# Down projection cut into steps between the next pair's gate_up chunks, in a mixture-of-experts loop on one core

## The chip, the core and the metric

One Trainium2 chip, one of its cores. A core has TensorE (PE: matmuls, and PEld: its weight loads), VectorE (DVE), ScalarE (ACT), GpSimd (POOL) and SyncE (SP), which here only issues transfers. The metric is the device time of one execution in microseconds, as the median of several runs; a profiled execution gives the trace, whose span is a little shorter than the execution's time.

## The reference

A decoder layer on 272 tokens (256 and 16 meta tokens) of width 2048: a mixer (mLSTM and sparse attention), then a hierarchical mixture of experts. Only the second half is touched by the change:

```python
h = layer_norm(ALPHA * h + mix, ln1_g, ln1_b)
# router: a group of 4, then the top 2 of its 8 experts: 32 experts, 2 per token
def run_block(args):
    toks, ws, e = args
    xb = x2[toks]
    gu = xb @ w_gate_up[e]                         # 2048 -> 1024
    hb = silu(gu[:, :D_FF]) * gu[:, D_FF:]         # 512
    return (hb @ w_down[e]) * ws[:, None]          # 512 -> 2048
...
h = layer_norm(ALPHA * h + ffn, ln2_g, ln2_b)
return h[:, N_META:]
```

All weights are float32: 8 MB of gate_up and 4 MB of down per expert, 403 MB for 32 experts, each used once.

## The kernel before

Only the 256 tokens that reach the output go through the experts. Each expert takes up to 64 rows (a loop behind the main one serves an expert with more, and runs only if there is one).

**Loads.** `specs` lists 386 loads in the order of use: for each pair of experts 16 gate_up chunks (256 rows of the weight, 1 MB each, `g`), then 8 down chunks (a quarter of an expert, 1 MB each). SP issues them (line 808) in a ring of 14 slots named by the tags of tiles that are dead by then (x0 to x3, y0 to y3, m0 to m3, u0, u1); two early chunks go into the accumulator's room instead. `issue()` issues the next load as soon as the slot that it takes has been used; `next_w()` hands out the next chunk.

**One pair of experts.** `expert_up` runs twice: 8 chunks, in each 2 values of k, and for each k two matmuls of 64 columns by 512, one into each half of the array's columns (lines 1078 and 1080). A float32 matmul is two instructions in the trace ("passes"). Behind the eighth chunk ScalarE applies silu (L1084), VectorE multiplies (L1085, `hb`), four transposes of 64 rows bring hb's columns to partitions (L1088, `ph`), and ScalarE copies them (L1091, `hT`). Then down runs for both experts, one into each half of the columns (L1242, `py`, four PSUM banks, 4 x 4 x 2 matmuls). The four results wait in `pend`; `flush(1)` behind each of the next chunks takes one: scaled by the gate into a high and a low part (L1231 `yh`, L1232 `yl`), scattered to tokens by a one-hot matmul (L1186, `pc`) and added to `acc` by VectorE (L1192): the combine.

**Around it.** `dispatch(q)` gathers the rows of four experts by one-hot matmuls into `xe` (L1002, evacuated by L1006 and L1009), ahead of every second pair; `slots_of` makes the one-hot of the way back. `add_residual(n)` adds a quarter of the residual in each of pairs 1 to 4, `final_scale` makes the last norm's scale during the last expert; both broadcast a row of 512 with `bcast_cols`: four diagonal matrices on VectorE and four matmuls with ones (L1104). `final_rows_load`, `final_masks` and `final_rows` prepare constants of the last norm. The last pair's down goes by columns (LASTP, L1254), each part combined at once, then the norm and eight output transfers.

**Order.** A list scheduler of the framework puts the instructions of each engine in order before the run: it takes the ready instruction that is first in the program, by its own estimate of times. An engine's queue is then run strictly in that order, so a matmul that isn't ready holds up those behind it.

## Time and profile before

| | us |
|---|---|
| runs | 1804.3, 1806.74, 1811.79; median 1806.74 |
| the profiled execution | 1807.82 |
| its span in the trace | 1806.1 |
| PE busy | 1718.2 (95%) |
| VectorE, ScalarE, GpSimd busy | 711.8, 455.6, 111.0 |
| loads of gate_up, 1 MB each: issue to landing, median | 15.0 |

The span is what the trace covers; 1.7 us of the execution lie outside of it. The busy time of PE counts overlapped passes once. The expert loop begins at about 816 us.

### The profile page before, as it was taken

To read this page: it belongs to the slowest core of one execution; us is meant where nothing else is said; L and a number is where in the kernel's file an instruction comes from. 1 tells how busy PE (TensorE), PEld (TensorE's weight loads), DVE (VectorE), ACT (ScalarE), POOL (GpSimd) and SP (SyncE) were. 2 spreads that over 40 slices of the span, in tenths; PEclk is the share of its full clock that TensorE was granted. 3 is DMA by queue.
4 is the path that set the end of the run, shared out by engine and by line. 5 is a ranking of instruction groups with operands and counts; after the bars stand their busy time and mean duration, and the time that the engine had idled before them with its cause. 6 is when DMAs were issued, how large, how long until landed. Compare 5 with 4: busy or idle time off the path is not lost. (4 is left out here: it accounts for less than half of the span.)

```text
span 1806.1 us, 21173 instructions
## 1 busy us (share of the span) xinstructions
PE 1718.2 (95%) x8626; PEld 1043.8 (58%) x8626; DVE 711.8 (39%) x1204; ACT 455.6 (25%) x703; POOL 111.0 (6%) x131
## 2 busy tenths in 40 slices
PE   8599999999999999999999999999999999999996
PEld 7598899988787877874343343333433434334332
DVE  7356774454556456552232242122112221222024
ACT  5243444444343444342010110110101101101010
POOL 3000210001122022000000000000000000000002
PEclk8799999999999999999999999999999999999998
DMA  7634454447565568458999999999999999999992
GB/s 219 129 117 142 141 164 140 148 156 247 173 213 173 198 217 295 171 212 343 419 403 408 413 356 421 421 391 421 421 420 420 422 420 421 420 422 420 421 402 71
DMA packets 155925, 538.67 MB, mean 298 GB/s; under 512 B 15772, under 2 KB 64116, under 8 KB 107680
## 3 DMA queue, kind: packets, MB, share of 16 engines
q1 hardware_dynamic: 153120, 530.54, 76.4%
q0 software_dynamic: 2640, 6.72, 1.9%
q8 instruction: 69, 1.13, 0.3%
q14 instruction: 32, 0.26, 0.0%
q10 hardware_dynamic: 64, 0.02, 0.0%
HBM read 533.50 MB, written 3.74 MB: 297 GB/s over the span
## 5 line engine op out<-in xcount | busy, mean ns | idle before, releaser
L1078 PE MATMUL gu<-we,xe 128*64 128x512 f32 x1016 | 455.9, 597 | 0.0
L1080 PE MATMUL gu<-we,xe 128*64 128x512 f32 x1016 | 454.5, 597 | 0.0
L1242 PE MATMUL py<-we,hT 128*64 128x512 f32 x960 | 276.8, 611 | 0.0
L1078 PEld LDWEIGHTS gu<-we,xe 128*64 128x64 f32 x1016 | 131.7, 137 | 244.2 <-issue 230.1
L1085 DVE TENSOR_TENSOR hb<-gu,hb 64x512 f32<-64x512 f32 x32 | 22.0, 689 | 349.1 <-ACT hb L1084 349.1
L1242 PEld LDWEIGHTS py<-we,hT 128*64 128x64 f32 x960 | 82.1, 137 | 123.8 <-issue 113.5
L1080 PEld LDWEIGHTS gu<-we,xe 128*64 128x64 f32 x1016 | 131.5, 137 | 17.2 <-issue 16.1
L1084 ACT ACTIVATE hb<-gu 64x512 f32<-64x512 f32 x32 | 18.9, 591 | 422.5 <-PE gu L1080 422.5
L1192 DVE TENSOR_TENSOR acc<-pc,acc 128x512 f32<-128x512 f32 (+1 forms) x122 | 77.5, 677 | 76.3 <-PE pc L1186 76.3
L1231 ACT ACTIVATE yh<-py,gsl 128x512 fp32r<-128x512 f32 (+1 forms) x65 | 42.7, 679 | 255.4 <-PE py L1242 178.7
L1232 DVE SCALAR_TENSOR_TENSOR yl<-py,gsl,yh 128x512 fp32r<-128x512 f32 (+1 forms) x65 | 46.7, 736 | 139.1 <-ACT yh L1231 138.7
L1009 DVE TENSOR_SCALAR xe<-pxe,gbp 128x256 f32<-128x256 f32 x64 | 34.8, 544 | 111.3 <-PE pxe L1002 111.3
L1002 PEld LDWEIGHTS pxe<-oh,uh 128*128 128x128 f32 x256 | 40.6, 197 | 48.3 <-DVE xe L1009 27.9
L1186 PE MATMUL pc<-yh,ohT 128*128 128x512 f32 (+1 forms) x130 | 53.9, 438 | 14.5 <-DVE acc L1192 11.6
L1006 ACT ACTIVATE xe<-pxe,gbp 128x256 f32<-128x256 f32 x64 | 36.0, 563 | 106.9 <-PE pxe L1002 106.9
L1002 PE MATMUL pxe<-oh,uh 128*128 128x256 f32 x256 | 59.6, 315 | 2.0 <-DMA acc<-in_w_gate_up_dram 2.0
L1178 POOL TENSOR_TENSOR fin<-acc,fin 128x512 f32<-128x512 f32 (+1 forms) x10 | 10.3, 1052 | 785.7 <-DVE acc L1192 785.7
L1186 PEld LDWEIGHTS pc<-yh,ohT 128*128 128x128 f32 x130 | 23.0, 188 | 55.6 <-issue 37.5
L1002 PE MATMUL pxe<-oh,ul 128*128 128x256 f32 x256 | 52.1, 285 | 0.0
L1186 PE MATMUL pc<-yl,ohT 128*128 128x512 f32 (+1 forms) x130 | 51.3, 418 | 0.8 <-DVE yl L1232 0.7
L1088 PEld LDWEIGHTS ph<-ident,hb 64*128 64x128 f32 x128 | 17.8, 210 | 44.3 <-DVE hb L1085 43.5
L1002 PEld LDWEIGHTS pxe<-oh,ul 128*128 128x128 f32 x256 | 41.1, 199 | 0.0
(920 smaller groups left out, 3109.7 us busy)
## 6 DMA issues: line engine op xcount, KB each, us to landing
we<-in_w_gate_up_dram SPq DMA_DIRECT2D x254, 1024.0 KB, 15.0
we<-in_w_down_dram SPq DMA_DIRECT2D x126, 1024.0 KB, 13.2
gm_r<-in_w_in_dram SPq DMA_DIRECT2D x16, 1024.0 KB, 5.0
ga_r<-in_w_in_dram SPq DMA_DIRECT2D x16, 1024.0 KB, 5.1
wo_r<-in_w_out_dram SPq DMA_DIRECT2D x16, 1024.0 KB, 5.1
qk_r<-in_w_in_dram SPq DMA_DIRECT2D x8, 1024.0 KB, 6.4
mv_r<-in_w_in_dram SPq DMA_DIRECT2D x8, 1024.0 KB, 5.3
aq_r<-in_w_in_dram SPq DMA_DIRECT2D x8, 1024.0 KB, 5.2
```

The lines of the kernel that those rows point to most:

```text
L1002: nc.tensor.matmul(pt[:, :4 * C], lhsT=part[:, b, rows_of(k)], rhs=ohf[:, b], start=i == 0 and b == 0, stop=i == 1 and b == 1)
L1006: nc.scalar.activation(xe[:, k], pt[:, :4 * C], AF.Identity, bias=gbp[:, 1, k:k + 1], scale=gbp[:, 0, k:k + 1])
L1009: nc.vector.tensor_scalar(xe[:, k], pt[:, :4 * C], gbp[:, 0, k:k + 1], gbp[:, 1, k:k + 1], op0=ALU.mult, op1=ALU.add)
L1078: nc.tensor.matmul(pg_[other], lhsT=lt, rhs=w[:, kk, 0:512], start=k == 0, stop=k == KD - 1)
L1080: nc.tensor.matmul(pg_[mine], lhsT=lt, rhs=w[:, kk, 512:1024], start=k == 0, stop=k == KD - 1)
L1084: nc.scalar.activation(hb[mine], pg_[other], AF.Silu)
L1085: nc.vector.tensor_tensor(hb[mine], pg_[mine], hb[mine], op=ALU.mult)
L1186: nc.tensor.matmul(pc[:, :n], lhsT=ohT[:, b * P:b * P + P], rhs=y[:, :n], start=i == 0, stop=i == 1)
L1192: nc.vector.tensor_tensor(av, pc[:, :n], av, op=ALU.add)
L1231: nc.scalar.activation(yh[:, :n], py[:, :n], AF.Copy, scale=gate)
L1232: nc.vector.scalar_tensor_tensor(yl[:, :n], py[:, :n], gate, yh[:, :n].bitcast(F32), op0=ALU.mult, op1=ALU.subtract)
L1242: nc.tensor.matmul(pys[c][i * 64:i * 64 + 64], lhsT=hTs[i][:, kk], rhs=ws[i][:, 0, c * 512:c * 512 + 512], start=kk == 0, stop=kk == 3)
```

## The change

- `specs` becomes a dictionary. From the second pair on, two down chunks of the pair before stand ahead of every fourth gate_up chunk.
- The ring becomes a free list: a chunk's slot is returned by `used()` when its last matmul is written, and the next load takes the oldest free slot. There are still 14 slots; the final scale and the constants no longer take slots of the ring, except one.
- `expert_up` is split. In the loop over 16 chunks of a pair: a chunk (`up_chunk`), then one sixteenth of the down of the pair before (`down_step`, two matmuls; none behind the first chunk, two behind the last), then a combine if two results wait (or in the first two chunks).
- The transposes are done once per pair for both experts (`up_turn`, 128 rows), behind the first chunk of the next pair.
- `dispatch` stands behind all of a pair's chunks, `slots_of` behind the eleventh chunk of every second pair.
- Rows of ln1 and ln2 are loaded after the first pair, split in two parts after the second, and broadcast with one matmul each (`bcast_rows`, 9 rows, float32r) instead of four diagonals and four matmuls. `add_residual` moves one pair later; `final_scale` moves behind the last chunk.

```diff
-    specs = []
-    for e0 in range(0, NE, 2):
-        for e in (e0, e0 + 1):
-            specs += [(w_gu[e, kc * 256:kc * 256 + 256].rearrange("(p k) c -> p k c", k=2), 2, 1024)
-                      for kc in range(8)]
-        if e0 + 2 < NE:
-            specs += [(w_dn[e].rearrange("(p k) c -> p k c", k=4)[:, kk:kk + 1], 1, D)
-                      for kk in range(4) for e in (e0, e0 + 1)]
-        else:
-            specs += [(w_dn[e, :, c0:c0 + n].rearrange("(p k) c -> p k c", k=4), 4, n)
-                      for c0, n in LASTP for e in (e0, e0 + 1)]
-    slots = [(big, t) for t in XT]
+    specs = {}
+    for p in range(NE // 2):
+        for n in range(16):
+            if p and n % 4 == 0:
+                kk = n // 4
+                for e in (2 * p - 2, 2 * p - 1):
+                    specs["d", e, kk] = (w_dn[e].rearrange("(p k) c -> p k c", k=4)[:, kk:kk + 1],
+                                         1, D)
+            e, kc = 2 * p + n // 8, n % 8
+            specs["g", e, kc] = (w_gu[e, kc * 256:kc * 256 + 256]
+                                 .rearrange("(p k) c -> p k c", k=2), 2, 1024)
+    for c0, n in LASTP:
+        for e in (NE - 2, NE - 1):
+            specs["l", e, c0] = (w_dn[e, :, c0:c0 + n].rearrange("(p k) c -> p k c", k=4), 4, n)
+    todo = deque(specs)
+    ndone = len(todo)
+    free = deque((big, t) for t in XT)
     live = {}
+    home = {}
     extra = {}
-    order = []
-    state = {"issued": 0, "used": 0}
-
-    def slot_tile(shape, name, r, dt=F32):
-        pool, tag = slots[r % NSLOT]
-        return pool.tile(shape, dt, name=name, tag=tag, bufs=1)
 
     def issue(n=None):
 
-        while state["issued"] < (len(specs) if n is None else n):
-            i = state["issued"]
-            r = len(order)
-            if i not in extra and r >= NSLOT and order[r - NSLOT] >= state["used"]:
+        while todo and (n is None or ndone - len(todo) < n):
+            key = todo[0]
+            if key not in extra and not free:
                 break
-            src, a, b = specs[i]
-            if i in extra:
-                w = extra[i]().rearrange("p (a b) -> p a b", a=a)
+            todo.popleft()
+            src, a, b = specs[key]
+            if key in extra:
+                w = extra[key]().rearrange("p (a b) -> p a b", a=a)
             else:
-                order.append(i)
-                w = slot_tile([P, a, b], f"we{i}", r)
+                home[key] = pool, tag = free.popleft()
+                w = pool.tile([P, a, b], F32, name="we" + "_".join(map(str, key)), tag=tag, bufs=1)
             nc.sync.dma_start(out=w, in_=src)
-            live[i] = w
-            state["issued"] = i + 1
-
-    def next_w():
-        i = state["used"]
-        state["used"] = i + 1
-        return live.pop(i)
-
-    NSLOT = 4 + 4 + 4 + 2
+            live[key] = w
+
+    def used(*key):
+
+        live.pop(key)
+        if key in home:
+            free.append(home.pop(key))
+
     ta_ctx.close()
-    slots += [(big, t) for t in YT] + [(mx, t) for t in MT] + [(up, t) for t in UT]
+    free += [(big, t) for t in YT] + [(mx, t) for t in MT]
+    NSLOT = len(free)
...
+    extra.update({("g", 1, NSLOT - 8 + i): lambda i=i: in_acc(i) for i in range(2)})
+    issue(NSLOT + 2)
+    free += [(up, t) for t in UT]
...
-    def expert_up(e, xe, hb):
+    hTs = {}
+
+    def up_chunk(e, kc, xe, pg_):
...
+        used("g", e, kc)
...
-        pt = pdt(f"ph{e}")
+
+    def up_turn(p, hb):
+
+        pt = pdt(f"ph{p}")
         for kk in range(4):
-            nc.tensor.transpose(pt[:, kk * C:kk * C + C], hb[mine, kk::4],
-                                ident[mine, mine])
-        hT = me.tile([P, 4, C], F32, name=f"hT{e}", tag="hT", bufs=2)
-        nc.scalar.copy(hT, pt[:, :256].rearrange("p (a b) -> p a b", a=4))
-        return hT
+            nc.tensor.transpose(pt[:, kk * P:kk * P + P], hb[:, kk::4], ident)
+        hT = me.tile([P, 4, P], F32, name=f"hT{p}", tag="hT", bufs=1)
+        nc.scalar.copy(hT, pt.rearrange("p (a b) -> p a b", a=4))
+        hTs[p] = hT
+
+    def down_step(p, kk, c, py):
+
+        for i in range(2):
+            nc.tensor.matmul(py[i * 64:i * 64 + 64], lhsT=hTs[p][:, kk, 64 - i * 64:128 - i * 64],
+                             rhs=live["d", 2 * p + i, kk][:, 0, c * 512:c * 512 + 512],
+                             start=kk == 0, stop=kk == 3)
+        if c == 3:
+            for i in range(2):
+                used("d", 2 * p + i, kk)
...
-    def bcast_cols(c0, name):
-
+    def bcast_rows(m, n, name):
+
+        dg = me.tile([P, P], F32R, name=f"{name}d", tag="dg", bufs=2)
+        nc.vector.tensor_copy(dg, mk[:, m:m + 1].to_broadcast([P, P]))
         pt = pdt(name)
-        for c in range(4):
-            dg = me.tile([P, P], F32, name=f"{name}d{c}", tag="dg", bufs=2)
-            nc.vector.tensor_scalar(dg, ident, col[:, c0 + c:c0 + c + 1], None, op0=ALU.mult)
-            nc.tensor.matmul(pt[:, c * P:c * P + P], lhsT=ones, rhs=dg, start=True, stop=True)
+        r = slice(32 * n, 32 * n + 9)
+        nc.tensor.matmul(pt, lhsT=dg[r], rhs=gr[r], start=True, stop=True)
...
-            nc.scalar.copy(fin[0][:, n * 512:n * 512 + 512], bcast_cols(104 + 4 * n, f"pg2{n}"))
+            nc.scalar.copy(fin[0][:, n * 512:n * 512 + 512], bcast_rows(2, n, f"pg2{n}"))
...
-    def final_rows_load():
+    mk = cst([P, 5], "mk")
...
-            for r, m, a in ((0, 3, ln2_g), (3, 2, ln2_b)):
+            for r, m, a in ((0, 3, ln2_g), (3, 2, ln2_b), (5, 2, ln1_g), (7, 2, ln1_b)):
...
+        mr = cst([P, 9], "mr")
+        for r in range(9):
+            late(nc.vector.tensor_reduce(mr[:, r:r + 1], idr[:, r], axis=AX.X, op=ALU.add))
+        late(nc.vector.tensor_tensor(mk[:, 0:1], mr[:, 1:2], mr[:, 4:5], op=ALU.add))
+        for r in (6, 8):
+            late(nc.vector.tensor_tensor(mk[:, 0:1], mk[:, 0:1], mr[:, r:r + 1], op=ALU.add))
+        for i, r in ((2, 0), (3, 5), (4, 7)):
+            late(nc.vector.tensor_tensor(mk[:, i:i + 1], mr[:, r:r + 1], mr[:, r + 1:r + 2],
+                                         op=ALU.add))
...
-    def final_rows():
+    def rows_split():
+        nonlocal gr
         h = me.tile([P, 512], F32R, name="grh", tag="yh")
-        gr = slot_tile([P, 512], "gr", NORD + 3, F32R)
+        gr = me.tile([P, 512], F32R, name="gr", bufs=1)
...
-    for pr_ in range(NE // 2):
-        e0 = 2 * pr_
-        q = pr_ // 2
...
+    turn = []
+    for p in range(NE // 2):
+        e0 = 2 * p
+        if p:
+            pys = [pyp.tile([P, 512], F32, name=f"py{p - 1}_{c}", tag="py") for c in range(4)]
+        steps = deque((kk, c) for kk in range(4) for c in range(4) if p)
+        for n in range(16):
+            e, kc = e0 + n // 8, n % 8
+            if kc == 0:
+                pg_ = pgu.tile([P, 512], F32, name=f"gu{e}", tag="gu")
+            up_chunk(e, kc, xe, pg_)
+            while turn:
+                turn.pop()()
+            for _ in range(0 if n == 0 else 1 if n < 15 else 2):
+                if steps:
+                    kk, c = steps.popleft()
+                    down_step(p - 1, kk, c, pys[c])
+                    if kk == 3:
+                        pend.append(lambda c=c, py=pys[c], f=gated_of(p - 1, cur):
+                                    f(c * 512, 512, py))
+            issue()
+            if n == 10 and p % 2:
+                cur = slots_of(p // 2, ohf)
+            if len(pend) > 1 or n < 2:
+                flush(1)
+            if n == 7:
+                hb = me.tile([P, 512], F32, name=f"hb{p}", tag="hb", bufs=1)
+            if kc == 7:
+                up_end(e, pg_, hb)
+            if n == 15:
+                turn.append(lambda p=p, hb=hb: up_turn(p, hb))
+        if p == 0:
+            prepare()
+            rows_load()
+            row_masks()
+        if p % 2:
+            q = p // 2
+            if p == LAST:
+                while turn:
+                    turn.pop()()
+                flush()
+            if q + 1 < NE // 4:
+                xe, ohf = dispatch(q + 1)
+        if p == 1:
+            rows_split()
+        if 2 <= p < 6:
+            add_residual(p - 2)
+
+    pool, tag = next(f for f in free if f[1] not in XT)
+    fin.append(pool.tile([P, D], F32, name="fin0", tag=tag, bufs=1))
+    f12 = me.tile([P, 2, D], F32, name="fin12", tag="xe", bufs=1)
+    fin += [f12[:, 0], f12[:, 1]]
+    final_scale()
...
```

## Rows read from the trace of the kernel before

**Rows 1.** The page: busy time of each engine, its share of the span and its instructions.

```profile
PE 1718.2 (95%) x8626; PEld 1043.8 (58%) x8626; DVE 711.8 (39%) x1204; ACT 455.6 (25%) x703; POOL 111.0 (6%) x131
```

**Rows 2.** Busy time by stage of the expert loop: start and end in us, length, busy us of PE, of PE's weight loads, VectorE, ScalarE and GpSimd, granted clock, DMA share, GB/s.

```profile
842.00:930.00 88.00, 87.45 (x397) 35.92 (x395) 19.08 (x37) 10.52 (x19) 0.00 (x0) 1.00 1.01 420
930.00:1000.00 70.00, 68.05 (x278) 25.51 (x276) 25.01 (x51) 6.51 (x11) 4.18 (x8) 0.98 1.00 397
1000.00:1070.00 70.00, 67.64 (x309) 28.35 (x305) 22.79 (x43) 9.75 (x17) 0.00 (x0) 1.00 0.97 389
1070.00:1140.00 70.00, 67.65 (x282) 25.07 (x284) 21.67 (x42) 4.57 (x8) 0.00 (x0) 1.00 1.01 411
1140.00:1210.00 70.00, 67.89 (x306) 27.49 (x302) 13.98 (x23) 9.66 (x17) 0.00 (x0) 1.00 0.99 401
1210.00:1700.00 490.00, 473.59 (x2082) 185.96 (x2082) 101.57 (x175) 55.86 (x99) 0.00 (x0) 1.00 1.01 421
```

**Rows 3.** Waits from 800 us to the end: engine, what and line, what it waited for, then us in total, times, longest us.

```profile
PEld gu L1078 <- DMA we<-in_w_gate_up_dram: 7.1, 24, 0.4
PE ph L1088 <- DVE hb L1085: 16.3, 29, 0.7
```

**Rows 4.** The load queue (SP, line 808) from 1700 to 1726 us: the issues with first and last start, and the time from issue to landing (least, median, most).

```profile
L808 SPq DMA_DIRECT2D we<-in_w_gate_up_dram x11: 327/328/328, 1699.7 to 1724.6; - x11
DMA to landing us min/median/max: 18.6/20.0/20.1
```

**Rows 5.** Timeline near the end of gate_up: start us, length us, engine, line, operation. The first pass of the last chunk.

```profile
1759.47 0.59 PE L1078 MATMUL gu<-we,xe 128*64 128x512 f32 x1
```

**Rows 6.** Groups of PE by line and shape from 1425.3 to 1543.1 us (two pairs of experts): line, engine, operation, tiles, shapes, count | busy us, mean ns | idle before.

```profile
L1078 PE MATMUL gu<-we,xe 128*64 128x512 f32 x129 | 57.7, 596 | 0.0
L1242 PE MATMUL py<-we,hT 128*64 128x512 f32 x128 | 35.5, 602 | 0.0
L1186 PE MATMUL pc<-yh,ohT 128*128 128x512 f32 x16 | 6.7, 440 | 1.6 <-DVE acc L1192 1.6
```

**Rows 7.** Timeline of PE at the end of a pair's second expert and the start of a dispatch: start us, length us, engine, line, operation, tiles, count, idle before.

```profile
1512.43 0.59 PE L1078 MATMUL gu<-we,xe 128*64 128x512 f32 x1
1512.44 0.59 PE L1080 MATMUL gu<-we,xe 128*64 128x512 f32 x1
1512.87 1.02 PE L1242 MATMUL py<-we,hT 128*64 128x512 f32 x2
1514.44 0.69 PE L1088 MATMUL ph<-ident,hb 64*128 64x64 f32 x4 [0.55 <-DVE hb L1085]
1515.06 0.51 PE L1002 MATMUL pxe<-oh,uh 128*128 128x256 f32 x2
...
1516.28 1.07 PE L1242 MATMUL py<-we,hT 128*64 128x512 f32 x2
```

**Rows 8.** Timeline of PE between a pair's first and second expert.

```profile
1144.97 0.59 PE L1078 MATMUL gu<-we,xe 128*64 128x512 f32 x1
...
1146.12 0.70 PE L1088 MATMUL ph<-ident,hb 64*128 64x64 f32 x4 [0.56 <-DVE hb L1085]
1146.75 0.64 PE L1078 MATMUL gu<-we,xe 128*64 128x512 f32 x1
```

**Rows 9.** Timeline of PE where down ends and the next gate_up begins, in the first pairs.

```profile
870.92 0.59 PE L1078 MATMUL gu<-we,xe 128*64 128x512 f32 x1
871.30 0.59 PE L1242 MATMUL py<-we,hT 128*64 128x512 f32 x1
871.35 0.59 PE L1078 MATMUL gu<-we,xe 128*64 128x512 f32 x1
871.73 0.59 PE L1242 MATMUL py<-we,hT 128*64 128x512 f32 x1
...
872.58 1.88 PE L1080 MATMUL gu<-we,xe 128*64 128x512 f32 x4
```

**Rows 10.** Timeline of PE at combines: the first behind down, the second inside gate_up.

```profile
1477.67 0.74 PE L1186 MATMUL pc<-yh,ohT 128*128 128x512 f32 x2
...
1478.81 0.64 PE L1078 MATMUL gu<-we,xe 128*64 128x512 f32 x1
...
1480.68 0.50 PE L1186 MATMUL pc<-yh,ohT 128*128 128x512 f32 x1
...
1482.68 0.64 PE L1078 MATMUL gu<-we,xe 128*64 128x512 f32 x1
```

**Rows 11.** Timeline of PE in the last expert, with the row broadcasts of final_scale.

```profile
1738.72 0.71 PE L1104 MATMUL pg<-pg20d,ones 128*128 128x128 f32 x4
...
1741.72 1.07 PE L1078 MATMUL gu<-we,xe 128*64 128x512 f32 x2
...
1744.79 0.64 PE L1078 MATMUL gu<-we,xe 128*64 128x512 f32 x1
```

**Rows 12.** Timeline of PE: the first full run of the last down.

```profile
1764.09 3.65 PE L1254 MATMUL py<-we,hT 128*64 128x512 f32 x16 [0.46 <-ACT hT L1091]
```

**Rows 13.** Single lines of the kernel: a 128x128 transpose (count: least/median/most ns, first and last start), a 5x512 matmul and a small reduction (count | busy us, mean ns | idle).

```profile
L849 PE MATMUL pu<-ident,u x32: 270/272/328, 732.0 to 804.2; 128*128 128x128 f32 x32
L1365 PE MATMUL pt<-gr,nmT 5*128 5x512 f32 x8 | 4.0, 748 | 1.0 <-DVE nmT L1360 0.6 <-DVE acc L1367 0.4
L1034 DVE TENSOR_REDUCE gsl<-pgt 64x2 f32<-64x4 f32 x16 | 2.5, 159 | 4.5 <-PE pgt L1029 4.4
```

More of the change, by code (lines that the diff above doesn't have):

```diff
@@ L1 @@
 import math
+from collections import deque
 from contextlib import ExitStack
@@ L1067, in flush @@
             pend.pop(0)()
[L1069 removed]
+    hTs = {}
+    def up_chunk(e, kc, xe, pg_):
         s0 = (e % 4) * C
         mine, other = [slice(i * 64, i * 64 + 64) for i in ((0, 1) if e % 2 else (1, 0))]
[L1072 to L1083 removed]
+        w = live["g", e, kc]
+        for kk in range(2):
+            k = kc * 2 + kk
+            lt = xe[:, k, s0:s0 + C]
+            nc.tensor.matmul(pg_[other], lhsT=lt, rhs=w[:, kk, 0:512], start=k == 0,
+                             stop=k == KD - 1)
+            nc.tensor.matmul(pg_[mine], lhsT=lt, rhs=w[:, kk, 512:1024], start=k == 0,
+                             stop=k == KD - 1)
+        used("g", e, kc)
@@ new lines, in gated @@
+            combine(nn, c0, n, yh, yl, cur[0][:, j], p == 0, p == LAST)
+        return gated
+    turn = []
[45 more added lines that the diff above has]
+            add_residual(p - 2)
@@ new lines, in trunk @@
+    pool, tag = next(f for f in free if f[1] not in XT)
[3 more added lines that the diff above has]
+    final_scale()
+    nm5 = me.tile([P, 2, 4, 32], F32, name="nm5", tag="hb", bufs=1)
+    nc.vector.memset(nm5, 1.0)
+    gated = gated_of(LAST, cur)
+    for c0, n in LASTP:
+        py = pyp.tile([P, 512], F32, name=f"py{LAST}_{c0}", tag="py")
+        for kk in range(4):
+            for i in range(2):
+                nc.tensor.matmul(py[i * 64:i * 64 + 64, :n], lhsT=hTs[LAST][:, kk, 64 - i * 64:128 - i * 64],
+                                 rhs=live["l", NE - 2 + i, c0][:, kk], start=kk == 0, stop=kk == 3)
+        gated(c0, n, py)
```

90 lines of the change are left out of this document (14 added, 76 removed).

## The prediction

> **What bounds the kernel now.** I read the page first, then the stages, then the waits of TensorE, then the transfer queue. The page shows TensorE (PE) busy for 95% of the span [rows 1], so any gap in it is small. The change touches only the expert loop, which runs from about 816 us to the last output, so I cut that into stages [rows 2]. The reader is to see two things there. From 1210 to 1700 us the transfers run at 421 GB/s, and PE is busy 473.6 of 490 us: both are close to full. From 930 to 1210 us the rate falls to 397, 389, 411 and 401 GB/s. Against 421 that is 4.0 + 5.3 + 1.7 + 3.3 = 14.3 us in which the transfers stood idle, with 0.2 us more from 842 to 930.
>
> Which of the two sets the pace is told by the waits: PE's weight loads waited for gate_up chunks 24 times, 7.1 us in all, never longer than 0.4 us [rows 3]. PE is not starved. The chunks lie ready: the last one of gate_up is issued at 1724.6 us and lands about 20.1 us later, at 1744.7 [rows 4], and PE comes to it at 1759.47 [rows 5]. So 14.8 us of stock is left at the end. PE sets the end now, and the transfers are the next limit close behind it: PE can come forward by the stock (14.8 us) plus the idle transfer time that earlier freed slots give back (at most 14.5 us). That is the frame of the sum: 29 us, whatever PE saves beyond it.
>
> **What PE saves.** In a stretch of two pairs (118 us) gate_up has 129 passes in one half of the columns, as many in the other, and down has 128 [rows 6]. Two passes in the two halves of the columns start together (1512.43 and 1512.44), and the next follows 0.43 us later [rows 7], so these 386 passes are worth 83 us at full pairing.
>
> (a) Transposes. After the second expert of a pair, gate_up ends at 1512.44 + 0.43 = 1512.87, and the next full-rate work begins at 1515.06; in these 2.19 us one lone down matmul (two passes, 0.43 us if paired) and four transposes are done, with an idle 0.55 us for hb [rows 7]. Loss: 1.76 us. After the first expert it is 1146.75 - 1145.40 = 1.35 us [rows 8]. That is 3.1 us a pair, and rows 3 name the wait. The new code has one group of four 128x128 transposes a pair, behind a whole gate_up chunk (8 passes, 1.72 us), which covers the time from the expert's last pass to the end of hb: that pass stands one pitch before the pass of 1144.97, at 1144.54, and the transposes start at 1146.12, 1.58 us later [rows 8]. A 128x128 transpose is in [rows 13], 0.27 us each with overlap; four of them lie between 0.6 and 1.1 us, and I take 1.0 with the change of array shape. Saving 2.1 us a pair, 34 us in all. If the cover fails, 0.55 us a pair comes back (9 us).
>
> (b) Down. Its 128 passes are busy for 35.5 us [rows 6] where 27.5 would do: 8 us. Some of it is the lone matmul in (a), some is matmuls that fill the gaps of dispatch alone ("x2" in 1.07 us, [rows 7]); the new code keeps that filling, with gate_up or down work. I take 3 us per two pairs as gone, since the two experts' rows now come together: 24 us. Bounds: 0 and 6 us.
>
> (c) Combine. Today the first of four runs between down and gate_up and takes 1.14 us (1477.67 to 1478.81); one inside gate_up takes 2.00 us (1480.68 to 1482.68) [rows 10]. In the new code all four stand between chunks: 0.8 us a pair more, 13 us.
>
> (d) Row broadcasts. final_scale breaks the last expert's chunks: around 1738.72 the pass pairs come apart (L1078 x2 alone in 1.07 us) between the transposed constants [rows 11]. That stretch takes 6.1 us up to 1744.79 for two chunk halves; with its second half some 7 us are lost, and the four add_residual some 10 us by the same groups of 8 passes. New: 12 single matmuls. None with 9 rows is in the trace; nearest are 5x512 at 0.75 us and a combine pass at 0.44 [rows 6, 13]. Bounds 0.25 and 1.0 us; I take 0.5, since the combine pass is the same size: 6 us. Net gain about 11 us.
>
> Sum for PE: 34 + 24 - 13 + 11 = 56 us; with the lower bounds of (a) and (b) 23 us.
>
> (e) Mixing down steps into gate_up chunks. The trace has one place where passes of both alternate: 870.92 and 871.35 for gate_up, 871.30 and 871.73 for down, 0.43 us per couple, no extra time [rows 9]. So I take 0 per step. The other bound is a lone pass pair, 0.43 us per step; it is the rival below.
>
> (f) Hidden edits. rows_load doubles the small transfers of POOL to 16 and moves them to pair 0; POOL has nothing behind them before the last pair. The 9 reductions of row_masks are like a 0.16 us reduction [rows 13], 2 us on VectorE, which is busy 19.1 of 88 us there [rows 2]. Without that cover they would cost some 2 us once. The free list keeps 14 slots; a down chunk is now held for four steps between chunks (4 x 2.6 = 10 us, not 3.5), so one or two slots fewer take transfers. SP carries nothing but these loads in the loop: behind a chunk that waits for a slot stands only the next chunk. A chunk of 1.05 MB takes 2.5 us at 421 GB/s, so 20 us to landing [rows 4] means 8 chunks in flight; two fewer are still enough.
>
> **The sum.** PE's 56 us is more than the 29 us that the transfers allow, so the end is set by transfers. The stock is used up in the second half, and PE then waits for chunks. Last gate_up chunk lands: 1744.7 - 14 (idle time returned) = 1731. Behind it PE has the chunk (1.7 us), two down steps (1.7), a combine (1 to 2), and a lag, because four landings of 2.5 us come in lumps with two down chunks: together 7, at 1738. Then transposes, the hT copy, two combines and the four row matmuls of final_scale, partly on top of one another: 4, at 1742. From the first pass of the last down to the end it is 1806.1 - 1764.09 = 42.0 us [rows 12], of which nothing is changed: 1784 minus some 2 us, as the waits after 1742 overlap. Span 1782, and with the 1.7 us between span and the profiled time 1784 us. The profiled execution (1807.8 us) lies 1.1 us above the median of the runs, well inside the 0.5% (9 us) that I take for no change. So -23.8 us, -1.3%.
>
> On the rate that this rests on, rows 2 show 421 GB/s for 490 us. The Trainium skill, HBM Reference, section Specifications, gives a core about 358 GB/s, and about 425 for a core that streams alone. By the rates of rows 2 some 374 MB pass from 842 us to the last gate_up chunk: 888 us at 421, 1044 us by the first figure, 880 us by the second (estimates from that page). By the first this change could gain nothing and the stage would be longer than it is, so the trace rules it out; by the second the sum would be 1776 us.
>
> **Rivals.**
> - PE stays the limit because the gains of (b) or (c) are smaller, or each step in the new mix costs about 0.1 us of re-pairing (240 steps, 24 us). PE then gains 10 to 20 us net: 1788 to 1798. For it: the lone matmuls of rows 7 come from the order in which instructions were queued, and that order is made anew. Chance 0.20.
> - Within 0.5%: the slots. If held down chunks stop the transfers again and again (each four-step hold of two chunks costs one landing of 2.5 us in half of the pairs, some 15 us) and tail work grows by 5 us, the gain is eaten: 1799 to 1816. Against it: 8 chunks in flight. Chance 0.11.
> - Slower: the pairing of down steps breaks inside gate_up, since a combine or transposes (whole array) fall between a step's two matmuls or a step queues behind one half of the columns. A broken step costs 0.43 us; 240 steps 103 us; after PE's 56 us of savings that is 1855 us. It decides from 0.25 us per step (240 x 0.25 = 60 us), where the time is back at 1808 to 1812. For it: 1.88 us for four passes of L1080 alone right after the mixed place [rows 9]. Against it: the mixed place itself, and that gate_up's chunks stay whole around the combines [rows 10]. Chance 0.09.
>
> **Numbers.** The forecast case (1773 to 1792) has 0.60. Its floor: no idle transfer time at all and a tail shorter by 8 us. The PE-limited case adds 0.20 and is nearly all faster by over 0.5%: faster 0.80, same 0.11, slower 0.09. The range of both, 1773 to 1801 us, holds 0.80; the likeliest case's own is 1773 to 1792.
>
> **What would show it.** In the profile after: half as many transposes, the wait of L1088 for hb gone; 421 GB/s from about 880 us on, with the dip between 930 and 1210 gone; waits of weight loads for gate_up chunks grown from 7 us to tens of us, above all after 1300 us; last gate_up landing near 1731; PE less busy than 95%. Wrong would be: the dip is still there and PE waits for no chunk (then PE is the limit, rival one), or down passes with a mean pitch well over 0.22 us (rival three).

## The result, and the profile after

The changed kernel takes 1792.98 us (median of six runs, 1791.21 to 1793.54); the kernel before, run beside it, 1808.61 us. The ratio is 0.9911, 95% interval 0.9894 to 0.9929: 0.9% faster where 1.3% was forecast. The profiled execution took 1793.54 us, its span is 1791.8 us.

The answer to [rows 1], the line of the page on busy times:

```profile
PE 1713.5 (96%) x8478; PEld 1053.3 (59%) x8478; DVE 705.9 (39%) x1180; ACT 454.1 (25%) x687; POOL 115.5 (6%) x139
```

The answer to [rows 2], the stages of the expert loop (length, busy us of PE, weight loads, VectorE, ScalarE, GpSimd, granted clock, DMA share, GB/s):

```profile
842.00:930.00 88.00, 87.04 (x394) 35.41 (x392) 20.54 (x52) 11.22 (x19) 8.36 (x16) 1.00 1.01 418
930.00:1000.00 70.00, 68.06 (x286) 25.70 (x284) 16.71 (x30) 4.97 (x8) 0.00 (x0) 1.00 0.98 404
1000.00:1070.00 70.00, 69.03 (x304) 29.02 (x302) 19.46 (x33) 8.97 (x16) 0.00 (x0) 1.00 1.01 419
1070.00:1140.00 70.00, 67.75 (x277) 25.03 (x275) 21.89 (x38) 7.05 (x11) 0.00 (x0) 1.00 1.01 420
1140.00:1210.00 70.00, 67.94 (x303) 28.64 (x299) 19.57 (x33) 9.67 (x17) 0.00 (x0) 1.00 1.01 419
1210.00:1700.00 490.00, 479.38 (x2024) 195.44 (x2024) 104.81 (x175) 54.18 (x89) 0.00 (x0) 1.00 1.01 420
```

From 1000 us on the transfers run at 419 to 420 GB/s without a dip; only 930 to 1000 us is left at 404. Yet TensorE is not less busy but more, 479 of 490 us. On its waits, the answer to [rows 3] from 800 us on (engine, what, for what: us in total, times, longest):

```profile
PEld ph L1096 <- DVE hb L1090: 18.4, 8, 2.3
PEld py L1104 <- DMA wed<-in_w_down_dram: 3.7, 6, 1.4
PEld gu L1081 <- DMA weg<-in_w_gate_up_dram: 2.7, 4, 1.4
PE ph L1096 <- DVE hb L1090: 11.3, 8, 1.4
```

The answer to [rows 4], the load queue from 1697 to 1722 us:

```profile
L810 SPq DMA_DIRECT2D weg<-in_w_gate_up_dram x8: 327/328/328, 1697.4 to 1719.7; - x8
```

and of the last of these loads alone, from 1719 to 1720.5 us:

```profile
DMA to landing us min/median/max: 20.0/20.0/20.0
```

The answer to [rows 5], the timeline of PE at the first two passes of the last chunk, and behind it the last pair's transposes and the first pass of the last down:

```profile
1740.85 0.59 PE L1081 MATMUL gu<-weg,xe 128*64 128x512 f32 x1
1740.86 0.59 PE L1083 MATMUL gu<-weg,xe 128*64 128x512 f32 x1
...
1744.15 0.75 PE L1096 MATMUL ph<-ident,hb 128*128 128x128 f32 x4 [1.42 <-DVE hb L1090]
...
1746.23 0.64 PE L1296 MATMUL py<-wel,hT 128*64 128x512 f32 x1
```

The last gate_up chunk is issued at 1719.7 us, lands at 1739.7 and is used 1.2 us later. The stock of 14.8 us is used up: TensorE follows the transfers.

For the experiments I read three times from each trace: the first pass of the first dispatch (where the expert loop starts), the landing of the last gate_up chunk, and the end of the span.

| kernel | median us | loop starts | start to last landing | landing to end |
|---|---|---|---|---|
| before | 1806.7 to 1809.0 | 813.0 | 931.7 | 61.4 |
| changed | 1793.0 | 815.2 | 924.5 | 52.1 |
| changed, no low part in the combine | 1791.0 | 813.0 | 923.3 | 52.8 |
| before, no low part in the combine | 1789.0 | 814.6 | 920.9 | 51.6 |
| before with row broadcasts | 1786.1 | 812.4 | 921.4 | 48.8 |
| changed with column broadcasts | 1805.3 | 812.5 | 935.9 | 56.1 |
| before with joint down loads | 1797.0 | 815.0 | 929.3 | 51.6 |
| changed, mixing undone | 1786.4 | 810.6 | 922.6 | 51.8 |
| changed, written order kept | 1792.2 | 811.7 | 923.9 | 53.4 |
| changed, steps behind dispatch | 1794.2 | 812.4 | 925.9 | 54.2 |
| changed, last pair's loads reordered | 1794.0 | 811.8 | 904.8 | 74.7 |
| mixing undone, final scale moved | 1785.0 | 814.9 | 921.2 | 48.7 |

The start of the loop differs by up to 4.6 us between executions whose code is the same up to there, so the third and fourth columns say more than the time of one trace.

### The profile page after: what moved, and what is told of

Its sections match the earlier page's. It is cut to its first block, busy times and chain, and to the rows that moved or that the text cites. A ratio compares the mean times of both kernels' runs of the same rounds, so it can differ in the third digit from the quotient of the medians.

```text
span 1791.8 us, 20692 instructions
## 1 busy us (share of the span) xinstructions
PE 1713.5 (96%) x8478; PEld 1053.3 (59%) x8478; DVE 705.9 (39%) x1180; ACT 454.1 (25%) x687; POOL 115.5 (6%) x139
## 5 line engine op out<-in xcount | busy, mean ns | idle before, releaser
L1081 PE MATMUL gu<-weg,xe 128*64 128x512 f32 x1016 | 465.9, 598 | 0.6 <-DMA weg<-in_w_gate_up_dram 0.6
L1083 PE MATMUL gu<-weg,xe 128*64 128x512 f32 x1016 | 463.6, 598 | 0.0
L1104 PE MATMUL py<-wed,hT 128*64 128x512 f32 x960 | 308.6, 597 | 0.6 <-DMA wed<-in_w_down_dram 0.6
L1081 PEld LDWEIGHTS gu<-weg,xe 128*64 128x64 f32 x1016 | 126.7, 137 | 188.6 <-issue 181.8
L1104 PEld LDWEIGHTS py<-wed,hT 128*64 128x64 f32 x960 | 97.8, 137 | 160.5 <-issue 155.1
L1083 PEld LDWEIGHTS gu<-weg,xe 128*64 128x64 f32 x1016 | 122.3, 136 | 64.9 <-issue 62.7
L1004 PE MATMUL pxe<-oh,uh 128*128 128x256 f32 x256 | 65.5, 333 | 9.0 <-DVE xe L1011 4.8
L1011 DVE TENSOR_SCALAR xe<-pxe,gbp 128x256 f32<-128x256 f32 x64 | 34.8, 544 | 92.4 <-PE pxe L1004 52.1
L1204 POOL TENSOR_TENSOR fin<-acc,fin 128x512 f32<-128x512 f32 (+1 forms) x10 | 10.3, 1054 | 896.8 <-DMA wel<-in_w_down_dram 887.2
L1212 PEld LDWEIGHTS pc<-yh,ohT 128*128 128x128 f32 x130 | 23.1, 191 | 55.5 <-issue 17.8
L1004 PE MATMUL pxe<-oh,ul 128*128 128x256 f32 x256 | 51.6, 284 | 0.0
L1212 PEld LDWEIGHTS pc<-yl,ohT 128*128 128x128 f32 x130 | 24.1, 190 | 12.3 <-issue 8.1
```

What stands on the lines that cost most here:

```text
L1004: nc.tensor.matmul(pt[:, :4 * C], lhsT=part[:, b, rows_of(k)], rhs=ohf[:, b], start=i == 0 and b == 0, stop=i == 1 and b == 1)
L1011: nc.vector.tensor_scalar(xe[:, k], pt[:, :4 * C], gbp[:, 0, k:k + 1], gbp[:, 1, k:k + 1], op0=ALU.mult, op1=ALU.add)
L1081: nc.tensor.matmul(pg_[other], lhsT=lt, rhs=w[:, kk, 0:512], start=k == 0, stop=k == KD - 1)
L1083: nc.tensor.matmul(pg_[mine], lhsT=lt, rhs=w[:, kk, 512:1024], start=k == 0, stop=k == KD - 1)
L1104: nc.tensor.matmul(py[i * 64:i * 64 + 64], lhsT=hTs[p][:, kk, 64 - i * 64:128 - i * 64], rhs=live["d", 2 * p + i, kk][:, 0, c * 512:c * 51 ...
L1212: nc.tensor.matmul(pc[:, :n], lhsT=ohT[:, b * P:b * P + P], rhs=y[:, :n], start=i == 0, stop=i == 1)
```

## The experiments

**Do the transfers set the end? Less work for TensorE, the same bytes.** The same edit in both kernels:

```diff
-            for i, y in enumerate((yh, yl)):
+            for i, y in enumerate((yh, yl) if last else (yh,)):
...
-                                 start=i == 0, stop=i == 1)
+                                 start=i == 0, stop=i == 1 or not last)
```

In the changed kernel:

> The changed kernel without the low part of the combine in pairs 0 to 14 (one scatter matmul instead of two; the output loses the low bits of the experts' sums). That takes some 110 of TensorE's passes of about 0.31 us, 30 to 35 us, and not one byte of the loads. Theory 1 (transfers now set the end): 0 to 5 us faster than the changed kernel, 1788 to 1793 us, since only the dip between 930 and 1000 us can be filled; last gate_up chunk lands within 5 us of 1740; TensorE's waits for chunks grow to some 30 us. Theory 2 (TensorE still sets the end and the used-up stock is a coincidence): 25 us or more faster, under 1768 us.

Measured: 1791.04 us, ratio to before 0.9912 (0.9893 to 0.9930): 2 us less than the changed kernel. In the kernel before:

> The kernel before without the low part of the combine in pairs 0 to 14 (the same part of the sums left out as in the run on the changed kernel). Some 30 to 35 us of TensorE's work go, no bytes. Theory 1 (TensorE set the end before, with 14.8 us of stock and 14.5 us of idle transfer time as the limit): 15 to 29 us faster than the kernel before, 1778 to 1793 us, the stock at the last gate_up chunk near zero. Theory 2 (TensorE and nothing else): 30 us or more faster. If the kernel before was bound by transfers all the same: under 5 us.

Measured: 1789.03 us, 0.9904 (0.9886 to 0.9921): 18 us less. So TensorE did set the end before and does not after the change. One part of the expectation failed: in the changed kernel the waits for chunks came to 24.4 us in the weight loads' rows (14.1 for gate_up, 10.3 for down), but to only 6.9 us in the rows of TensorE's matmuls, although it had some 30 us less to do. Its matmuls took longer instead: down's 960 passes were busy for 319.8 us where the changed kernel has 308.6. The written-order run below shows how.

**What does TensorE need by itself? Fewer bytes, the same work.** In the changed kernel (the kernel before likewise, with one chunk taken for both):

```diff
-                for e in (2 * p - 2, 2 * p - 1):
+                for e in (2 * p - 2, 2 * p - 1)[:1 if p < 15 else 2]:
...
-                             rhs=live["d", 2 * p + i, kk][:, 0, c * 512:c * 512 + 512],
+                             rhs=live["d", 2 * p + (i if p == 14 else 0), kk][:, 0, c * 512:c * 512 + 512],
...
```

> The changed kernel with half of the down loads left out in pairs 0 to 13: both experts of a pair use the first one's down chunk, so 56 chunks of 1 MB (140 us at 2.5 us each) are not loaded, and TensorE does all of its work (the output is that of other weights). It shows what TensorE needs by itself. Theory 1: faster than the changed kernel, since transfers bound it; if TensorE's saving was the 56 us of the sum, the time is 1807 - 56 = 1751 us, if only just what the transfers allowed, 1780. Theory 2 (TensorE sets the end): within 5 us of the changed kernel.

Measured: 1762.39 us (0.9754, 0.9736 to 0.9771).

> The kernel before with the same 56 down chunks left out (both experts of a pair use the first one's down chunk in pairs 0 to 13). Both theories: TensorE set the end before, so at most 7 us faster (its waits for chunks), 1799 to 1807 us. The difference between this run and the changed kernel with the same chunks left out is what TensorE itself gained by the change: 56 us by the sum of the prediction, 23 us by its lower bounds.

Measured: 1761.65 us (0.9752, 0.9735 to 0.9769). A miss: 45 us faster where 7 were allowed, in a kernel that TensorE bounds. The edit did more than take bytes away: with one chunk for both experts their down matmuls become ready at once, and the order was made anew from that. The page's group of down's 960 passes shows it (busy us, mean ns). In the kernel before:

```profile
L1242 PE MATMUL py<-we,hT 128*64 128x512 f32 x960 | 276.8, 611 | 0.0
```

With the shared chunk:

```profile
L1242 PE MATMUL py<-we,hT 128*64 128x512 f32 x960 | 249.9, 602 | 0.0
```

That is 27 of the 45 us; how the rest divides was not tested. Two pairs take 111.6 us there (dispatch to dispatch, 1369.4 to 1480.9) against 117.7 before (1397.3 to 1515.1). So the two runs don't give the 56 us of the sum. They do compare the two loops with down well paired in both: of the 128 passes of down in such a stretch 6 start alone in the old loop with the shared chunk (no other pass within 0.15 us) and 10 in the changed one, where the kernel before has 24. The old loop takes 111.6 us per two pairs, the changed one 114.4 (1363.1 to 1477.5). Apart from the pairing, the new loop as it is scheduled costs TensorE 2.8 us more per two pairs; it saves nothing.

**Is it the pairing? Both experts' rows in one down load.**

```diff
-            specs += [(w_dn[e].rearrange("(p k) c -> p k c", k=4)[:, kk:kk + 1], 1, D)
-                      for kk in range(4) for e in (e0, e0 + 1)]
+            specs += [(w_dn[e0:e0 + 2].rearrange("e (p k) c -> p k e c", k=4)[:, kk, :, h:h + 1024], 2, 1024)
+                      for kk in range(4) for h in (0, 1024)]
...
-                                         rhs=ws[i][:, 0, c * 512:c * 512 + 512], start=kk == 0,
+                                         rhs=ws[c // 2][:, i, c % 2 * 512:c % 2 * 512 + 512], start=kk == 0,
```

> The kernel before, with each down load cut the other way: one load of 1 MB holds the rows of both experts of the pair for half of the columns (two runs of 4 KB a partition instead of one of 8 KB), so the two matmuls that should run side by side get their data at once. Bytes, matmuls and loop order stay. Theory 1 (down ran at 0.29 us a pass and not 0.215 because the order put the two experts' matmuls behind two landings): 0.24 to 0.25 us a pass, 40 us of TensorE's time less, so that the transfers set the end: 1787 to 1794 us. Theory 2 (a pass of down is slow for another reason): 0.29 us a pass and 1805 to 1809 us. If runs of 4 KB load slower: a rate under 415 GB/s from 1210 us on, and 1810 us or more.

Measured: 1796.96 us, 0.9941 (0.9918 to 0.9964): 11 us less, where 14 to 21 were expected. Down's group on its page:

```profile
L1242 PE MATMUL py<-we,hT 128*64 128x512 f32 x960 | 257.4, 607 | 1.9 <-DMA we<-in_w_down_dram 1.1
```

Its long stage:

```profile
1210.00:1700.00 490.00, 469.90 (x2100) 180.97 (x2098) 102.32 (x176) 56.38 (x98) 0.00 (x0) 1.00 1.02 417
```

Down's busy time fell by 19 of the 27 us, so most of its loss came from the two experts' rows lying in two loads. It came by the order made from that and not by waiting: in the kernel before, TensorE is never idle ahead of down (the 0.0 at the end of its row). But the down loads, now in runs of 4 KB, land every 2.56 us where gate_up's runs of 8 KB land every 2.49 (medians from 1210 us on): some 8 us for 120 loads, and 417 GB/s in the stage instead of 421. As a version it gains less than the next one; as a test the sign is clear, the size not.

**Which part of the change gives the gain? The row broadcasts alone.** `bcast_rows`, `rows_load`, `row_masks`, `rows_split` and `add_residual` of the change in the kernel before; in its loop:

```diff
         if pr_ == 0:
             prepare()
+            rows_load()
+            row_masks()
...
-        if 0 < pr_ < 5:
-            add_residual(pr_ - 1)
-        if pr_ == 2:
-            final_rows_load()
-        elif pr_ == 6:
-            final_masks()
+        if pr_ == 1:
+            rows_split()
+        if 2 <= pr_ < 6:
+            add_residual(pr_ - 2)
```

> The kernel before with the row broadcasts of the change alone (loads, masks, split, add_residual one pair later; final_scale stays in the last expert). Theory 1 (the broadcasts stop TensorE and with it the transfers in pairs 1 to 5; two pairs with them took 126 to 128 us, those without 117.7): 17 us of TensorE's time come back there and some 5 in the last expert, the dip of the transfer rate between 930 and 1210 us goes, and the time is 1789 to 1794 us: this part alone gives nearly all that the whole change gives. The prediction's size (11 us): 1796 us. Theory 2 (the gain comes from transposes and paired down steps): at most 5 us faster, 1802 us or more.

Measured: 1786.09 us, 0.9882 (0.9861 to 0.9904): 7 us faster than the whole change. The stages:

```profile
930.00:1000.00 70.00, 67.25 (x277) 24.75 (x275) 23.62 (x41) 7.20 (x12) 0.00 (x0) 1.00 1.01 420
1000.00:1070.00 70.00, 68.06 (x305) 27.79 (x303) 20.66 (x35) 9.07 (x16) 0.00 (x0) 1.00 1.01 419
1070.00:1140.00 70.00, 67.51 (x292) 24.49 (x290) 17.12 (x31) 5.52 (x10) 0.00 (x0) 1.00 1.01 420
1140.00:1210.00 70.00, 68.05 (x308) 27.73 (x306) 17.58 (x30) 9.07 (x16) 0.00 (x0) 1.00 1.01 419
```

Against [rows 2], the dip is gone: two pairs with a residual took 127.7 and 126.1 us before (dispatch to dispatch from 908.1) and take 119.6 and 120.4 now. The other way round, the change without its broadcasts (ln1's rows are then not loaded either):

```diff
-        pg1 = bcast_rows(3, n, f"pg1{n}")
+        pg1 = bcast_cols(72 + 4 * n, f"pg1{n}")
...
-        pb1 = bcast_rows(4, n, f"pb1{n}")
+        pb1 = bcast_cols(88 + 4 * n, f"pb1{n}")
...
-            nc.scalar.copy(fin[0][:, n * 512:n * 512 + 512], bcast_rows(2, n, f"pg2{n}"))
+            nc.scalar.copy(fin[0][:, n * 512:n * 512 + 512], bcast_cols(104 + 4 * n, f"pg2{n}"))
```

> The changed kernel with the old column broadcasts (four diagonals, four matmuls each) in add_residual and final_scale; all else as changed. Theory 1: the transfers stand idle again in pairs 2 to 5 for about 10 us and nothing makes that up, since from 1210 us on they run at their limit: 1800 to 1806 us. By the prediction's sum TensorE has 27 us to spare over what the transfers allow, so the loss of 11 us of them costs nothing: 1791 to 1795 us.

Measured: 1805.28 us, 0.9987 (0.9976 to 0.9999). The dip is back, although `add_residual` stands one pair later here too, so its place was not what removed it:

```profile
930.00:1000.00 70.00, 67.19 (x282) 26.28 (x280) 18.14 (x36) 4.51 (x8) 0.00 (x0) 0.98 0.96 395
1000.00:1070.00 70.00, 69.03 (x302) 29.62 (x299) 21.15 (x39) 9.40 (x16) 0.00 (x0) 1.00 0.94 385
```

Everything in the change but the broadcasts is worth 0.1%. My sum, by which TensorE had 27 us to spare, is refuted.

**Where does the rest lose 7 us? The mixing undone.** Rows, joint transposes and free list stay; down is one block again:

```diff
-            while turn:
-                turn.pop()()
-            for _ in range(0 if n == 0 else 1 if n < 15 else 2):
-                if steps:
-                    kk, c = steps.popleft()
-                    down_step(p - 1, kk, c, pys[c])
...
+        up_turn(p, hb)
...
+            for kk in range(4):
+                for c in range(4):
+                    down_step(p, kk, c, pys[c])
+                issue()
```

> The changed kernel with the mixing undone: a pair's down chunks are loaded behind its gate_up chunks and its 16 steps run as one block behind dispatch, as before; row broadcasts, joint transposes (right behind the pair's last chunk) and the free list stay. The rows alone gave 1786 us, the whole change 1793 us. Theory 1 (the 7 us are lost by the mixing: a dispatch with nothing to fill it stops the transfers at 930 to 1000 us, and the tail is longer): 1782 to 1788 us, 420 GB/s from 842 us on. Theory 2 (joint transposes or the free list lose them): 1791 to 1795 us.

Measured: 1786.38 us, 0.9879 (0.9848 to 0.9910): as fast as the rows alone, and all of its runs (1783.98 to 1789.36) lie below those of the change. By the medians, then, the mixing loses the 7 us, not the transposes or the free list. The traces show less of it. From the start of the loop to the end the change takes 976.6 us, this run 974.4 and the rows alone 970.2 (sums of the table): only 2.2 us between the first two, and the other 4.6 of their profiled executions lie ahead of the loop, in code that is the same. Whether the mixing costs all 7 us is therefore not shown.

Between the change and the rows alone, 6.4 us apart, the traces show two places. One is dispatch. With rows alone the order fills each pause of its 8 passes with down; in the changed kernel nothing is left to fill most of them with. The timeline of PE with the rows alone:

```profile
1153.20 0.51 PE L1002 MATMUL pxe<-oh,uh 128*128 128x256 f32 x2
1153.55 0.41 PE L1002 MATMUL pxe<-oh,ul 128*128 128x256 f32 x2
1153.79 0.40 PE L1002 MATMUL pxe<-oh,uh 128*128 128x256 f32 x2
1154.03 0.40 PE L1002 MATMUL pxe<-oh,ul 128*128 128x256 f32 x2
1154.36 1.08 PE L1250 MATMUL py<-we,hT 128*64 128x512 f32 x4
```

The timeline of PE in the changed kernel:

```profile
1145.88 0.52 PE L1004 MATMUL pxe<-oh,uh 128*128 128x256 f32 x2 [0.65 <-DVE xe L1011]
1146.23 0.41 PE L1004 MATMUL pxe<-oh,ul 128*128 128x256 f32 x2
1146.52 0.51 PE L1004 MATMUL pxe<-oh,uh 128*128 128x256 f32 x2
1146.87 0.40 PE L1004 MATMUL pxe<-oh,ul 128*128 128x256 f32 x2
...
1154.24 1.07 PE L1081 MATMUL gu<-weg,xe 128*64 128x512 f32 x2
```

From 1145.88 to 1154.24 us 48 passes of dispatch run alone, and in that time no chunk is used and no slot returned. At the dispatch of 899 us this shows in the load queue, the timeline of SP from 906 to 941 us:

```profile
906.62 2.46 SPq L810 DMA_DIRECT2D wed<-in_w_down_dram  x2
919.32 11.44 SPq L810 DMA_DIRECT2D weg<-in_w_gate_up_dram  x4
938.20 0.80 SPq L810 DMA_DIRECT2D wed<-in_w_down_dram  x2
```

No load is issued for 10.2 us up to 919.32, and again for 7.4 us up to 938.20. In the second pause TensorE runs a block of down, by the timeline of PE:

```profile
930.23 5.37 PE L1104 MATMUL py<-wed,hT 128*64 128x512 f32 x22
```

Then the transfers run out, in the stage from 935 to 940 us:

```profile
935.00:940.00 5.00, 5.00 (x26) 2.27 (x24) 0.00 (x0) 0.00 (x0) 0.00 (x0) 1.00 0.56 190
```

That is the dip of 404 GB/s: (420 - 404) / 420 x 70 = 2.7 us. It follows both pauses; what each does by itself was not tested. The other place is the end: 52.1 us behind the last landing against 48.8. The mixing has little to do with it, since 51.8 are left without it; the last run below finds most of it in the place of the final scale.

**Can dispatch be filled again?** Eight of the sixteen steps of every second pair behind it:

```diff
-            for _ in range(0 if n == 0 else 1 if n < 15 else 2):
+            for _ in range(n % 2 if p % 2 and p < LAST else 0 if n == 0 else 1 if n < 15 else 2):
...
                 xe, ohf = dispatch(q + 1)
+                while steps:
+                    kk, c = steps.popleft()
+                    down_step(p - 1, kk, c, pys[c])
...
```

> The changed kernel with 8 of the 16 steps of every second pair kept back and put behind the dispatch, so that the scheduler can fill the dispatch with them; loads in the same order, the down chunks of those steps held longer. Theory 1 (the mix took the fillers from the dispatch: 0.170 us a pass against 0.146 before, and the transfers idle while it runs): 0.145 to 0.155 us a pass, no dip at 930 to 1000 us, 1786 to 1790 us. Rival (the held slots stop the transfers instead): a rate under 415 GB/s in several stretches and 1795 us or more.

Measured: 1794.18 us, 0.9922 (0.9893 to 0.9951). A miss: dispatch still takes 0.17 us a pass, start to start, and in place of one dip there are two, 408 GB/s from 930 and 409 from 1070 us. The steps were issued ahead of dispatch's main part, not within it; what order would fill it stays open.

**Does the order made anew cost?** Gate_up and down matmuls held as written, by wrapping them:

```diff
...
-            nc.tensor.matmul(py[i * 64:i * 64 + 64], lhsT=hTs[p][:, kk, 64 - i * 64:128 - i * 64],
-                             rhs=live["d", 2 * p + i, kk][:, 0, c * 512:c * 512 + 512],
-                             start=kk == 0, stop=kk == 3)
+            late(nc.tensor.matmul(py[i * 64:i * 64 + 64],
+                                  lhsT=hTs[p][:, kk, 64 - i * 64:128 - i * 64],
+                                  rhs=live["d", 2 * p + i, kk][:, 0, c * 512:c * 512 + 512],
+                                  start=kk == 0, stop=kk == 3))
```

> The changed kernel with the matmuls of gate_up and down held in the order in which they are written (a chunk, then one step of both experts, and so on); nothing else moves. Theory 1 (the order made anew puts four steps of one expert behind one landing, so one half of the columns runs alone; as written the halves stay side by side): down near 0.23 us a pass from 1035 to 1635 us or wherever TensorE is not held by a landing, and since transfers set the end only the early dip and the tail can gain: 1786 to 1792 us. Rival (the scheduler's order was the better one: as written, TensorE stands at chunks that have not landed, and dispatch loses its last fillers): 1795 to 1805 us.

Measured: 1792.15 us, 0.9915 (0.9885 to 0.9944), as the change. But the picture of TensorE is another. The stage from 1210 us:

```profile
1210.00:1700.00 490.00, 447.42 (x2014) 173.40 (x2012) 99.77 (x165) 54.18 (x88) 0.00 (x0) 0.97 1.01 420
```

The longest of TensorE's waits in this stage:

```profile
PE gu L1081 <- DMA weg<-in_w_gate_up_dram: 31.7, 15, 5.3
```

The timeline of PE at a step between two chunks:

```profile
1463.72 0.59 PE L1081 MATMUL gu<-weg,xe 128*64 128x512 f32 x1
1463.73 0.59 PE L1083 MATMUL gu<-weg,xe 128*64 128x512 f32 x1
1464.15 1.03 PE L1104 MATMUL py<-wed,hT 128*64 128x512 f32 x4
1465.01 0.59 PE L1081 MATMUL gu<-weg,xe 128*64 128x512 f32 x1
```

The timeline of PE at the same place in the changed kernel as it is:

```profile
1463.23 0.59 PE L1083 MATMUL gu<-weg,xe 128*64 128x512 f32 x1
1463.65 4.08 PE L1104 MATMUL py<-wed,hT 128*64 128x512 f32 x13
1467.15 0.64 PE L1081 MATMUL gu<-weg,xe 128*64 128x512 f32 x1
```

Down's group on the page of the changed kernel:

```profile
L1104 PE MATMUL py<-wed,hT 128*64 128x512 f32 x960 | 308.6, 597 | 0.6 <-DMA wed<-in_w_down_dram 0.6
```

As written, a step's four passes take 0.86 us (1464.15 to 1465.01): two full pairs. As scheduled, 13 passes take 3.50 us, 0.27 each. The first four of them run alone, 0.43 us each; the same timeline up to 1465.1 us:

```profile
1463.65 1.88 PE L1104 MATMUL py<-wed,hT 128*64 128x512 f32 x4
```

From 1465.37 us on passes of the second expert start beside them. The chunk that these read had landed at 1457.7, so the order kept them back and not a landing. Over the whole loop 234 of down's 960 passes start alone (no other within 0.15 us), as written none. The Trainium skill, "TensorE: Matmul & The Clock Gate", section "Part 3: Packing small matmuls", has matmuls start and end strictly in queue order; the rows agree, the idle half is not filled from behind. Down is busy for 308.6 us against 247.7 as written. That is where the surplus is: 31.7 us of open waiting as written, hidden in slower matmuls as scheduled. As the transfers set the end, the time is the same.

**And the end?** The last pair's 16 gate_up chunks ahead of the down chunks of pair 14:

```diff
-            if p and n % 4 == 0:
+            if p and p < NE // 2 - 1 and n % 4 == 0:
...
+    for kk in range(4):
+        down_spec(NE // 2 - 1, kk)
     for c0, n in LASTP:
...
-            for _ in range(0 if n == 0 else 1 if n < 15 else 2):
+            for _ in range((0 if n < 15 else 16) if p == LAST else 0 if n == 0 else 1 if n < 15 else 2):
...
```

> The changed kernel with the last pair's loads in another order: its 16 gate_up chunks first, then the 8 down chunks of the pair before, then the last down by columns; the steps of pair 14 stand behind the last chunk. Same bytes and matmuls. Theory 1 (transfers set the end, and 52 us lie behind the last gate_up landing because down, transposes and combines of two pairs wait for it): that chunk lands 20 us earlier, near 1720, the last load still near 1761, and TensorE has little left behind that one: 1782 to 1787 us. Rival: TensorE starves on the 16 chunks (0.8 us each, 12 us) and has as much left at the end: 1790 to 1796 us.

Measured: 1793.96 us, 0.9926 (0.9903 to 0.9950): as the rival had it. The landing did come 23 us earlier, at 1716.6, but then, in the timeline of PE:

```profile
1718.03 0.59 PE L1087 MATMUL gu<-weg,xe 128*64 128x512 f32 x1
1719.18 21.16 PE L1108 MATMUL py<-wed,hT 128*64 128x512 f32 x64 [0.55 <-DMA wed<-in_w_down_dram]
1740.27 0.72 PE L1216 MATMUL pc<-yh,ohT 128*128 128x512 f32 x2
```

The 64 passes of down go at the pace of their eight landings, 21 us where 14 would do, and combines, transposes and final scale still lie behind 1740. Last, the mixing undone and the final scale put back among the last pair's chunks:

```diff
             up_chunk(e, kc, xe, pg_)
+            if p == LAST and n > 6 and not fin:
...
+                    final_scale()
...
```

> The run with the mixing undone, and in it the final scale moved back from behind the last chunk into the last pair's chunks. Theory 1 (with the transfers saturated from 842 us to the end, only the stretch behind the last gate_up landing is left; the final scale's four broadcasts and copies lie in it and are worth 2 to 3 us): 1782 to 1785 us, 48 to 50 us from that landing to the end instead of 51.7. Rival (they are hidden behind the wait for the last down loads): 1785 to 1788 us, as without the move.

Measured: 1785.04 us, 0.9862 (0.9840 to 0.9884). The stretch behind the last landing is 48.7 us as expected, 3.0 less than with the final scale in it. By its median it is the fastest kernel here that loads all the weights, 8 us ahead of the change, but its runs (1782.95 to 1786.70) overlap those of the rows alone (1784.41 to 1786.72): these two can't be told apart.

## Why the prediction was right, and where it was not

- **The number.** The median of 1793.0 us lies in the stated range, 1773 to 1801, and 1 us above that of the likeliest case, 1773 to 1792. In part this is luck: of TensorE's 56 us, (a) and (b) gave nothing that could be measured, and (d), put at 11, gave more than the whole change kept. The time also lies in the 1788 to 1798 of the first rival, whose condition did not hold: with 120 of TensorE's passes taken out the changed kernel is only 2 us faster.
- **What bounds.** Right. TensorE set the end before, the transfers set it after; the frame of 29 us held, and of the stock of 14.8 us all but 1.2 was used up.
- **The sum.** The span came out 9.8 us over the forecast of 1782. The mis-sized term is the idle transfer time given back: the last landing was to come 14 us earlier. From the start of the loop it came 931.7 - 924.5 = 7.2 us earlier. The rows alone reach 10.3: even without a dip the rate is 420 and not the 421 that I took, some 2 us in 920. Another 3 are, for the most part, the dip of 2.7 us behind the dispatch of 899 us; 1 to 2 stay unexplained. Beyond that the loop began 2.2 us later in this execution. This is not the change's doing: the code is the same up to there, and from 567 to 578 us the granted clock was 0.53 on average, most of that stretch at 1.2 GHz, where the kernel before had 0.84. The tail took 52.1 us where 51 were forecast.
- **(a), (b), (c).** The steps named for TensorE's gain failed. With the changed order (a) and (b) gave nothing that could be measured (1805.28 us without the broadcasts); (c) was not measured by itself. Transposes are fewer, but the wait for hb, which was to be gone, came 8 times, 11.3 us. In (b) I took it that dispatch keeps its filling; it takes as long as before (17.8 us from first to last pass, 17.9 before), with 48 of its 64 passes alone. Down, which (b) was to pair, has more passes alone than before, 234 and not 192. Held as written, TensorE has a surplus as I had counted on, but the transfers leave it no use.
- **(d).** Undersized. The guess of 0.5 us for a broadcast matmul was fair: two of them take 0.66 us (1157.41 to 1158.07). But the old groups had cost two pairs with a residual 10.0 and 8.4 us over the 117.7 of others, 18 us and not 10, and they stood in just the stretch where TensorE held up the transfers. This term alone, with the four broadcasts of the final scale, gives 21.6 us in the kernel before.
- **(e).** Zero per mixed step is right as written (0.86 us) and wrong as scheduled (13 passes, 3.50 us). The rival that the order is made anew had the right mechanism, but it decides only where TensorE sets the end.
- **(f).** Right: nothing of the hidden edits shows. The slots did bind once, at the dispatch of 899 us and the block of down behind it.
- **The signs.** 421 GB/s from 880 us on: nearly, but for 404 in one stage. Waits for chunks of tens of us and TensorE less busy: wrong, 2.7 us and 96%. I took a busy engine for a needed one.

The Trainium skill, "DMA: Bandwidth & Descriptors", section Bandwidth, has 425 GB/s for a transfer of 16 MB by a core whose neighbour is idle; the 417 to 420 of the runs above that are bound by transfers come close to it. No run shows whether another order of the same loads would reach more.

Open: what puts the order of dispatch right in the mixed loop; how much of the 7 us the mixing costs, since the traces show 2.2; and how the 3.3 us at the end divide between final scale (3.0 by the last run) and combines.

## What to carry to other kernels

When two limits lie within 2% of each other, ask of every part of a change in which stage it works: twelve broadcasts, eight of them in the one stretch where the engine held up the transfers, gave all of the gain, and a rebuilt loop, with most of its length where transfers were already full, gave none; the whole change is 7 us slower than the broadcasts alone. Busy time is no need: an order that lets half of the array run alone shows as 96% busy, and holding the written order is the cheap test of how much of it is surplus. And before fillers are moved, look at whom they fill: here down steps covered dispatch.

## What the runs showed of the hardware

- The same 960 passes of down keep TensorE busy for 308.6 us (changed), 276.8 (before), 257.4 (joint loads), 249.9 (shared chunk) or 247.7 (written order). Of them 234, 192, 118, 62 and 0 start with no other pass within 0.15 us.
- Loads of 1 MB in two runs of 4 KB a partition landed every 2.56 us, those in one run of 8 KB every 2.49 us, in the same execution (joint down loads, medians from 1210 us on).
- With pauses of up to 5.3 us for chunks, in the written order, the mean granted clock from 1210 to 1700 us was 0.97 (all but some 6% of the stage at 2.4 GHz, the rest at 1.2) where it was 1.00 in the changed kernel, and the mean pass of gate_up 612 ns where it was 598.
